# One more gate chunk before the shift columns, two shift tiles fewer on TensorE, a two-product low-rank chunk, and a query chunk behind linear attention

## The chip, the core and the metric

The kernel runs on one core of a Trainium2 chip. Its time is the device time of one execution in microseconds (us). Three runs of the kernel before took 2047.29, 2050.56 and 2052.04 us, with 2050.56 as their median. The trace is that of one further execution, which took 2051.18 us; from its first to its last instruction, its span, it took 2049.4 us.

The profile's names for the engines: PE is TensorE's matmul side and PEld its load of stationary blocks; DVE is VectorE, ACT is ScalarE, POOL is GpSimd, and SP is SyncE, which only issues DMAs here. Each engine works through its own instructions in the order in which they were written.

## What is computed

The reference is a trunk of two layers on 640 tokens, 128 of a context and 512 of a latent grid, with a model width of 2048. Both groups of tokens use the same weights; they differ in the conditioning vector that modulates them.

```python
for l in range(DEPTH):
    shift, scale, gate = modulation(c, ada_w[l], ada_b[l])     # silu(c) @ w + b, in three
    h = rms_norm(x, norm_g[l]) * (1.0 + scale) + shift
    if l % 2 == 0:      # even layer: attention || bidirectional gated linear attention (GLA)
        y, side = even_mixer(h, w_in_even[e], ...)
    else:               # odd layer: neighbourhood attention || spatial gating
        y, side = odd_mixer(h, w_in_odd[o], ...)
    x = x + gate * (y @ w_out[l])
y = rms_norm(x, final_norm_g)
```

In the even layer, `h @ w_in_even` gives eight attention queries, two keys and two values of 128 columns, the queries, keys and values of four GLA heads, 32 low-rank columns `r` from which the GLA gates `log_sigmoid(r @ wg + bg) / 16` are made, and 2048 gate columns; the mixers' output is multiplied with the SiLU of the gate columns. Everything is float32.

## The kernel before

**The matmuls.** Activations lie transposed: 16 blocks of 128 features by 640 tokens. A float32 product is made of three matmuls in a rounded type: both operands are split into a high part, which is the operand rounded, and a low part, which is the rest, and high x high, high x low and low x high are added up in a PSUM bank. The high parts are rounded by ACT (`acth`, `whi`), the low parts subtracted by POOL or DVE (`actl`, `wlo`). A *chunk* is 128 output columns of a weight: 16 blocks of the contraction, two halves of 320 tokens, three products, so 96 matmuls, all issued through one helper at L449 (`mm_k` calls it). The *shift* of the modulation is not added to the activations; it stands beside them as two extra columns (one of the context, one of the latent tokens), so that the second half of a chunk has 322 columns and the shift's part comes out as two columns of the bank. A chunk's result leaves its bank by three DVE instructions: `arena<-bank,rstd 128x320` for each half, which multiplies by the tokens' reciprocal norm, and `bc<-bank 128x2` for the two shift columns. The two halves alternate every four blocks and three banks rotate over them, so the bank of a chunk's first half is wanted again 24 matmuls after that half is complete.

**The start.** The modulation of layer 0 has to be made first. Its scales are 16 *tiles*: two 512 KB loads each (`Y<-ada`, `more<-ada`), 32 records in the profile at L1605 (16 matmuls with a stationary block of 32 columns, each in two records), a copy, and a matmul `small,adas` of two columns. The shifts' 16 blocks are made in two ways. `BOTH` = 8 of them are such tiles too. The other 8 are done by row: 256 KB loads (`raw<-ada_s`, four to a block, with a ring of five buffers), which DVE multiplies with the conditioning rows and adds up (`adas,old<-raw,bank`, a custom instruction with the read-out of its sum), once for each of the two conditioning vectors; some of the second are done by POOL (`prod<-raw,mixrow`) and ACT. When the last row is in, a few DVE additions, a rounding on ACT and a subtraction on DVE (`actl<-old,acth`, L1255) give the two shift columns. Until they exist, PE can work on chunks whose shift part is made elsewhere: the first `FIRST` = 6 gate chunks (columns 320 in both halves; their shift part is reduced from other loads, `gateT`, on DVE) and the first half of the low-rank chunk. The order of PE's work here is: matmuls of the gate chunks with tiles in between, the low-rank chunk's first half, then a transposition `ident,old` of the shifts and the low-rank chunk's second half, the first with 322 columns.

**After it** come the 16 GLA chunks (k, q and two v for each of four heads), each evacuated into elementwise work of its head: on DVE four `TENSOR_SCALAR`, a product, a scan over the tokens, another product and a backward scan, in an order that the planner sets; a gate chunk (gate 14) is the filler while the last GLA head ends, then k, v and the eight queries of the attention with the attention heads in between, and the other gate chunks. The out-projection of each layer and the chunks of the odd layer are done in pairs with Strassen's method, whose sums of weight or activation blocks are made by ACT, DVE and POOL. At the border to layer 1 the new activations are normed, scaled (`rs<-rs,A`, `adas<-adas,A`), rounded (`acth`) and split (`actl`) while PE works.

**What sets the order.** A planner in the program simulates the engines when the kernel is built: the class `Pace` holds a cost for each kind of instruction, generators of side work are spawned, and after every few matmuls `tick` lets them write their next instructions. `until` makes a generator wait until an operand would be there, `calm(x)` until ACT and DVE have at most so much work queued, and `need` makes PE's side run the others until a flag is set. Nothing of that runs on the chip; it fixes the order of each engine's queue. In `units`, where a chunk's matmuls are written, it stands so:

```python
for j in range(k, k + 4):
    if p[half] is not done:
        self.mm_k(c, j, [(p[half], half)], k0)
    if j % 2:
        self.tick(2)
```

Of the kernel before, what the change touches and what calls it, by code (L numbers as in the profile page):

```python
# [50 lines left out]
LEAD, FIRST = 1, 6  # L51
CUT, AGAIN, KEPT = 384, (10, 2), (8, 0)
BOTH = 8
# [192 lines left out]
class Trunk:  # L246
# [425 lines left out]
    def strassen_jobs(self, c1, c2, last, unit):  # L672
# [25 lines left out]
        add = lambda o, a, b, op: ("add", lambda: (piece(o), piece(a), piece(b)), op, 4 in (o, a, b))  # L698
# [9 lines left out]
        if ns == ALL:  # L708
            after = {("A12", 8): [add1], ("S1", 5): [add2], ("S2", 5): [add3], ("S4", 5): [add4]}
            assert all(t in [k + m for k, m in self.blocks_of(ns, f)] for f, t in after)  # L710
        else:
            after = {("A12", 6): [add1, add2], ("S1", 6): [add3], ("S2", 6): [add4]}
# [41 lines left out]
    def wpump(self, force=False):  # L754
# [107 lines left out]
    def mm_k(self, c, k, outs, first=0, last=KT - 1, r=0):  # L862
# [4 lines left out]
        todo = []  # L867
# [117 lines left out]
    def spair(self, c1, c2):  # L985
# [70 lines left out]
        end = self.steps(c1, c2)[-1]  # L1056
        for key in self.steps(c1, c2):
            f = key[1]
            if len(key) == 3 and key[0] == c1:
# [10 lines left out]
            elif f == "S1":  # L1070
                plus(full(xa), x)
                ev1(xa, None)
                self.drop(xa)
                v = take()
                self.need("T124")
                product(v, full, f, tt(0))
            elif f == "S2":
                product(t, full, f, tt(1))
                x = copy(half(t))
                plus(x, half(v))  # L1080
            elif f == "S4":
# [4 lines left out]
                self.drop(xb)  # L1086
            elif f == "S3":
# [2041 lines left out]
```

## Time and profile before

| | |
|---|---|
| median of three runs | 2050.56 us (2047.29 to 2052.04) |
| the profiled execution | 2051.18 us, span 2049.4 us |
| mean granted TensorE clock | 0.996 |
| busy: PE, DVE, ACT, POOL | 2012.4, 1356.0, 1098.7, 1362.9 us |
| matmul records | 14255 |
| moved by DMA | 344.13 MB, 168 GB/s on average |

How to read it: busy time is the time in which an engine has an instruction in work. Matmuls overlap, so one that is listed with 0.31 us starts 0.15 us after the one before it; the distance of two starts, not the listed duration, is what a matmul costs. In the waits, a row names the engine that waits with its instruction's operand and line, behind the arrow what ended the wait, and then the sum in us, the number of waits and the longest. In the timeline's rows stand the start and the duration in us, the instruction with its shapes, and in brackets the idle time before it with what ended it. In the table of stretches of time, each engine's busy time (and instructions) stands in the order PE, PEld, DVE, ACT, POOL, then the granted clock, the share of time that the 16 DMA engines were busy, and GB/s.

### The profile page before, as it was taken

What the parts mean: (1) busy time and instruction counts of PE and PEld (TensorE: products, weight loads), DVE (VectorE), ACT (ScalarE), POOL (GpSimd) and SP (SyncE); (2) the same over time, 40 slices, a digit from 0 to 9 for tenths busy, and PEclk for the clock granted to TensorE, in tenths of its full rate; (3) what the DMA queues carried; (4) which work ended last, traced back from release to release, by engine and by line L of the source; (5) the groups of instructions that cost most, each with busy time, mean ns of one, the idle gap of its engine ahead of it and who ended that gap; (6) DMA issues with size and microseconds to landing.
All of it is one profiled execution on the core that took longest, in us unless ns stands there. A gap on an engine that the chain in (4) does not pass through costs nothing.

```text
span 2049.4 us, 40331 instructions
## 1 busy us (share of the span) xinstructions
PE 2012.4 (98%) x14255; PEld 1976.9 (96%) x14255; DVE 1356.0 (66%) x3175; ACT 1098.7 (54%) x2430; POOL 1362.9 (67%) x1096
## 2 busy tenths in 40 slices
PE   8999999999999999999999999999999999999997
PEld 6899999999999999999989999999999999999997
DVE  4656677476557666898577787656665677568444
ACT  5445555445564766544465444565565654455443
POOL 5555465446556555798755777766766688878884
PEclk9999999999999999999999999999999999999999
DMA  9965433336456455577534434444344354265437
GB/s 376 400 208 163 143 112 102 121 119 185 156 184 215 148 179 179 174 242 230 186 107 138 134 126 132 133 132 130 120 147 126 120 174 154 91 216 194 144 98 277
DMA packets 234316, 344.13 MB, mean 168 GB/s; under 512 B 22049, under 2 KB 139649, under 8 KB 234113
## 3 DMA queue, kind: packets, MB, share of 16 engines
q1 hardware_dynamic: 232912, 340.38, 50.7%
q8 instruction: 112, 1.84, 0.4%
q10 hardware_dynamic: 1200, 1.17, 0.2%
q14 instruction: 92, 0.75, 0.1%
HBM read 304.99 MB, written 33.85 MB: 165 GB/s over the span
## 4 chain that ended last, share of the span: by engine, by line
PE 87%; DMA 6%; DVE 3%; ACT 2%; issue 1%; POOL 1%; SPq 0%; DVEq 0%; POOLq 0%; ACTq 0%
PE bank L449 84%; PE bank L454 2%; DMA more<-ada 1%; DMA Y<-ada 1%; DVE bank L219 1%; DVE arena L219 1%; DVE Y L219 1%; DMA arena<-yT_dram 1%; PE bank L1605 0%; DMA Y<-xT 0%; ACT acth L219 0%; DMA wraw<-w_even 0%; DMA wraw<-w_out 0%; DVE rs L219 0%; DMA rawx<-ada_g 0%
## 5 line engine op out<-in xcount | busy, mean ns | idle before, releaser
L449 PE MATMUL bank<-acth,whi 128*128 128x320 f32 (+3 forms) x3072 | 941.0, 318 | 6.8 <-DVE bc L219 2.8
L449 PE MATMUL bank<-actl,whi 128*128 128x320 f32 (+3 forms) x3072 | 917.0, 310 | 1.3 <-POOL actl L219 1.3
L449 PE MATMUL bank<-acth,wlo 128*128 128x320 f32 (+3 forms) x3072 | 915.6, 310 | 0.0
L219 POOL TENSOR_TENSOR wlo<-wraw,whi 128x512 fp32r<-128x512 f32 (+2 forms) x415 | 531.3, 1290 | 395.3 <-ACT whi L219 360.4
L449 PEld LDWEIGHTS bank<-acth,whi 128*128 128x128 f32 (+1 forms) x3072 | 569.1, 188 | 14.7 <-issue 4.1
L449 PEld LDWEIGHTS bank<-actl,whi 128*128 128x128 f32 (+1 forms) x3072 | 569.6, 188 | 3.5 <-POOL actl L219 1.5
L449 PEld LDWEIGHTS bank<-acth,wlo 128*128 128x128 f32 (+1 forms) x3072 | 568.6, 188 | 0.8 <-POOL wlo L219 0.6
L219 POOL TENSOR_TENSOR wlo<-rs,whi 128x384 fp32r<-128x384 f32 (+2 forms) x370 | 457.7, 1262 | 111.4 <-ACT whi L219 78.5
L219 ACT ACTIVATE whi<-wraw 128x512 fp32r<-128x512 f32 (+2 forms) x425 | 245.8, 586 | 164.1 <-PE bank L449 85.2
L219 ACT ACTIVATE whi<-rs 128x384 fp32r<-128x384 f32 (+2 forms) x370 | 191.9, 536 | 100.8 <-PE bank L449 45.7
L449 PE MATMUL bank<-eh,whi 128*128 128x322 f32 (+1 forms) x666 | 209.5, 314 | 0.0
L449 PE MATMUL bank<-el,whi 128*128 128x322 f32 (+1 forms) x666 | 206.4, 310 | 0.0
L449 PE MATMUL bank<-eh,wlo 128*128 128x322 f32 (+1 forms) x666 | 206.3, 310 | 0.0
L219 POOL TENSOR_TENSOR prod<-adas,mixrow 128x512 f32<-128x512 f32 x93 | 121.1, 1313 | 50.6 <-ACT prod L219 32.4
L219 DVE TENSOR_TENSOR bank<-bank,sums 128x320 f32<-128x320 f32 (+1 forms) x148 | 70.1, 495 | 95.8 <-ACT sums L219 47.9
L449 PEld LDWEIGHTS bank<-eh,whi 128*128 128x128 f32 x666 | 125.4, 188 | 0.0
L449 PEld LDWEIGHTS bank<-eh,wlo 128*128 128x128 f32 x666 | 125.4, 188 | 0.0
L449 PEld LDWEIGHTS bank<-el,whi 128*128 128x128 f32 x666 | 125.3, 188 | 0.0
L219 DVE CUSTOM_DVE_ANT_0 adas<-adas,bank,part 128x512 bf16<-128x512 f32 x146 | 108.6, 744 | 22.6 <-DMA adas<-ada 15.7
L219 POOL TENSOR_TENSOR wlo<-adas,whi 128x512 fp32r<-128x512 f32 x62 | 80.2, 1300 | 44.0 <-ACT whi L219 43.5
L219 ACT ACTIVATE sums<-bank 128x320 f32<-128x320 f32 (+1 forms) x111 | 48.2, 434 | 103.6 <-PE bank L449 97.4
L219 DVE CUSTOM_DVE_ANT_0 adas<-adas,bank 128x512 bf16<-128x512 f32 x107 | 73.2, 684 | 13.6 <-DMA adas<-ada 5.2
(287 smaller groups left out, 3057.6 us busy)
## 6 DMA issues: line engine op xcount, KB each, us to landing
wraw<-w_even SPq DMA_DIRECT2D x176, 256.0 KB, 3.3
rs<-w_odd SPq DMA_DIRECT2D x150, 256.0 KB, 3.3
adas<-ada SPq DMA_DIRECT2D x128, 256.0 KB, 3.8
adas<-ada_g SPq DMA_DIRECT2D x64, 256.0 KB, 3.8
rs<-w_out SPq DMA_DIRECT2D x60, 256.0 KB, 3.7
adas<-w_odd SPq DMA_DIRECT2D x50, 256.0 KB, 3.8
Y<-ada SPq DMA_DIRECT2D x24, 512.0 KB, 7.7
more<-ada SPq DMA_DIRECT2D x24, 512.0 KB, 7.8
```

Source lines behind the costliest of these rows:

```text
L219: return f(*args, **kw)
L449: self.nc.tensor.matmul(out, lhsT, rhs, start=start, stop=stop, **kw)
L454: self.nc.tensor.transpose(out, in_, self.ident[:k, :k])
```

## The change

1. `FIRST` goes from 6 to 7: gate chunk 14 is now one of those without a shift column and runs in the start.
2. `BOTH` goes from 8 to 6: two of the shift tiles leave PE, and the shifts of 10 blocks instead of 8 are reduced from row loads: 40 loads of 256 KB instead of 32, and 4 of 512 KB fewer.
3. The low-rank chunk's weight has its 32 columns four times in a stationary block of 128 columns, one of them replaced by the low part. Two matmuls replace three: the block with the activations' high part (128 columns), and 32 high columns with their low part. The chunk has 64 matmuls instead of 96; the 128 rows of its result take over the parts that the small gate product needs (`gla_wg`, `gla_rank`).
4. Query chunk 0 takes the filler's place behind the GLA chunks, in a third buffer beside the gates'; attention head 0 is spawned as soon as the first value chunk is done.
5. `units` ticks after every block of the contraction, with 1 and 2 in turn, where it ticked 2 after every second.
6. In the Strassen pairs that end a run of pairs, the products come in another order (S2, S1, S3, S4, A22, or S3 ahead of the second plain block), the sums with them, and one sum is written in two halves.
7. At the border, the split of a block waits for `calm(1.5)` while the last block isn't rewritten yet, where it waited for `calm(3.0)`.
8. The reciprocal root of a GLA head's norm is written out, with an `until` between ACT's and DVE's part.

```diff
-LEAD, FIRST = 1, 6
+LEAD, FIRST = 1, 7
-BOTH = 8
+BOTH = 6
@@ strassen order
         if self.count[c1] == ALL:
-            return names("A11", "A12", "S1", "S2", "S4", *(("S3", "A22") if c1 in self.ends else ("A22", "S3")))
-        return [*names("A11"), (c1, PLAIN, 0), *names("A12", "S1", "S2", "S4"), (c2, PLAIN, 0), *names("S3", "A22")]
+            return names("A11", "A12", *(("S2", "S1", "S3", "S4", "A22") if c1 in self.ends else ("S1", "S2", "S4", "A22", "S3")))
+        last = [*names("S3"), (c2, PLAIN, 0)] if c1 in self.ends else [(c2, PLAIN, 0), *names("S3")]
+        return [*names("A11"), (c1, PLAIN, 0), *names("A12", "S1", "S2", "S4"), *last, *names("A22")]
...
         if m < M:
-            raw = raw[:, :, None, :].to_broadcast([128, n, M // m, m])
-            hi, lo = (x.rearrange("p a (b c) -> p a b c", c=m) for x in hl)
-        nc.scalar.activation(hi, raw, AF.Copy)
+            hi, lo = hi.rearrange("p a (b c) -> p a b c", c=m), hi[:, :, 0:m]
+            nc.scalar.activation(hi, raw[:, :, None, :].to_broadcast([128, n, M // m, m]), AF.Copy)
+            hi, hl = lo, [hl[0], hl[0]]
+        else:
+            nc.scalar.activation(hi, raw, AF.Copy)
...
+            if m < M:
+                n = h.shape[1]
+                self.mm(p[:M, :n], hi, h, start=k == first, stop=k == last, skip_group_check=True)
+                self.mm(p[:m, :n], hi[:, m : 2 * m], l, start=False, stop=k == last, skip_group_check=True)
+                continue
             todo += [(0, p, hi, h, k == first, False), (1, p, hi, l, False, False), (2, p, lo, h, False, k == last)]
...
-                    if j % 2:
-                        self.tick(2)
+                    self.tick(1 + j % 2)
...
-            yield from self.calm(self.calms[1])
+            yield from self.calm(self.calms[1] if f"{ready}:{order[-1]}" in self.flags else 1.5)
...
-        self.rsqrt(rs, sq, sq2)
+        self.act(rs, sq, AF.Ln)
+        self.act(rs, rs, AF.Exp, scale=-0.5)
+        yield from self.until(rs)
+        nc.vector.scalar_tensor_tensor(sq2, rs, -0.5, rs, ALU.mult, ALU.mult)
...
-        add(d["w_rb"], 96, True, None, lazy("vt", rows=96, then=lambda x: self.spawn(self.gla_rank(x))))
+        add(d["w_rb"], 128, True, None, lazy("vt", then=lambda x: self.spawn(self.gla_rank(x))))
...
-        gp_first(14)
+        add(wE[0], 128, True, None, lazy("hq", SC, pre=("gla_elem3",), then=lambda x: L.update(q0=x)))
...
                 self.spawn(work())
+                if kv == 0:
+                    self.spawn(self.even_head(0, L["q0"], L["k0"], v, L["sw"].next(), "eq0"))
...
-            for h in range(4 * kv, 4 * kv + 4):
+            for h in range(4 * kv or 1, 4 * kv + 4):
```

Three places in the engines' orders. In these rows an instruction's line, its kind, what it writes and reads, and its shape are given; x4 means four of it in a row.

**SP, the last loads of the tiles.** Before:

```order
L492 DMA raw_297<-crow_b 128x512
L492 DMA raw_298<-ada_s 128x512
L492 DMA raw_299<-ada_s 128x512
L492 DMA Y<-ada 128x1024
L492 DMA more_126<-ada 128x1024 x3
L492 DMA wraw<-w_even 128x512
L492 DMA wraw<-w_rb 128x128
L492 DMA raw_300<-ada_s 128x512
```

With the change:

```order
L492 DMA wraw<-w_even 128x512
L492 DMA more_126<-ada 128x1024 x2
L492 DMA raw_296<-ada_s 128x512
L492 DMA wraw<-w_even 128x512
L492 DMA Y<-ada 128x1024 x2
L492 DMA raw_297<-ada_s 128x512
L492 DMA raw_298<-ada_s 128x512
L492 DMA raw_299<-ada_s 128x512
```

Both pieces hold the last load of a tile (`more_126<-ada` before, `Y<-ada` with the change). Up to it the queue has issued 42.75 MB before and 39.86 MB with the change. Behind it stand 14 rows of `ada_s` and two of `crow_b` (the conditioning rows) before, and 23 and four with the change. On PE, 188 matmuls of 320 columns stood between the last tile's `small,adas` and the transposition `ident,old` of the shifts, and now 292; in all, 620 matmuls of 320 columns stood ahead of that transposition, and now 702.

**DVE, the third GLA head (head 2) and the evacuation of the next chunk** (`bank_68` and `bank_69` are its halves). Before:

```order
L219 TENSOR_SCALAR Y<-bank_72,small 128x320
L219 TENSOR_TENSOR Y<-Y,arena_1683 128x640
L219 SCALAR_TENSOR_TENSOR arena_1683<-arena_1683,Y 128x640
L219 TENSOR_TENSOR Y<-Y 128x640
L219 SCALAR_TENSOR_TENSOR Y<-arena_1683,Y 128x640
L219 TENSOR_TENSOR arena_1683<-bank_68,rstd 128x320
L219 TENSOR_SCALAR bc_3507<-bank_68 128x2
L219 TENSOR_TENSOR arena_1683<-bank_69,rstd 128x320
```

With the change:

```order
L219 TENSOR_SCALAR Y<-bank_72,small 128x320
L219 TENSOR_TENSOR Y<-Y,arena_1768 128x640
L219 SCALAR_TENSOR_TENSOR arena_1768<-arena_1768,Y 128x640
L219 TENSOR_TENSOR arena_1768<-bank_68,rstd 128x320
L219 TENSOR_SCALAR bc_3600<-bank_68 128x2
L219 TENSOR_TENSOR arena_1768<-bank_69,rstd 128x320
L219 TENSOR_TENSOR arena_1768<-arena_1768 128x640 x2
L219 TENSOR_TENSOR Y<-Y 128x640
```

The evacuation stood behind the second scan (the second `SCALAR_TENSOR_TENSOR`); it now stands ahead of the product `Y<-Y` and of that scan. On PE, 49 matmuls lay between the head's last small gate product and the bank's next use, and now 40.

**ACT, the border to layer 1** (`rs`, `adas`: blocks that are scaled; `eh`: a rounding of another sum, which waits for DVE). Before:

```order
L219 ACTIVATE acth<-rs_8045 128x640
L219 ACTIVATE whi<-wraw 128x512
L219 ACTIVATE eh_8043<-bank_69 128x320
L219 ACTIVATE adas<-adas,A_97 128x128
L219 ACTIVATE adas<-adas,A_97 128x512
L219 ACTIVATE acth<-adas 128x640
```

With the change:

```order
L219 ACTIVATE rs_8048<-rs_8048,A_97 128x128
L219 ACTIVATE rs_8048<-rs_8048,A_97 128x512
L219 ACTIVATE acth<-rs_8048 128x640
L219 ACTIVATE whi<-wraw 128x512
L219 ACTIVATE adas<-adas,A_97 128x128
L219 ACTIVATE adas<-adas,A_97 128x512
L219 ACTIVATE acth<-adas 128x640
```

The `eh` no longer stands between the two blocks, and the scaling of the `rs` block, which DVE did before for this block (`rs<-rs,A`), is on ACT.

More of the change, by code (lines that the diff above doesn't have):

```diff
@@ L709, in strassen_jobs @@
             after = {("A12", 8): [add1], ("S1", 5): [add2], ("S2", 5): [add3], ("S4", 5): [add4]}
+            if c1 in self.ends:
+                after = {("A11", 8): [add1], ("A12", 4): [add2], ("S2", 5): [add3], ("S1", 5): [add(4, 3, 2, ALU.subtract, (0, 4))], ("S1", 8): [add(4, 3, 2, ALU.subtract, (4, 8))]}
             assert all(t in [k + m for k, m in self.blocks_of(ns, f)] for f, t in after)
@@ L866, in mm_k @@
         hi, lo = (x[:, i, :] for x in self.wget((c, u, r)))
-        todo = []
+        todo, m = [], w.shape[2]
         for p, half in outs:
@@ L1056, in spair @@
         end = self.steps(c1, c2)[-1]
+        done = set()
         for key in self.steps(c1, c2):
             f = key[1]
+            done.add(key)
             if len(key) == 3 and key[0] == c1:
@@ L1069, in spair @@
                 product(xa, full, f, M(x1))
[L1070 to L1080, printed above, removed]
+            elif f in ("S1", "S2"):
+                if xa:
+                    plus(full(xa), x)
+                    ev1(xa, None)
+                    self.drop(xa)
+                    xa = None
+                    self.need("T124")
+                if f == "S1":
+                    v = take()
+                    product(v, full, f, tt(0))
+                else:
+                    product(t, full, f, tt(1))
+                    x = copy(half(t))
+                if {(c1, "S1"), (c1, "S2")} <= done:
+                    plus(x, half(v))
             elif f == "S4":
@@ L1086, in spair @@
                 self.drop(xb)
+                if (c1, "S3") in done:
+                    x = copy(full(t))
+                    self.drop(t)
             elif f == "S3":
@@ L1091, in spair @@
                     self.spawn(self.unfold(ns), first=True)
+                if xb is None:
+                    continue
                 x = copy(full(t))
@@ L2002, in gla_wg @@
         nc, wg, ws = self.nc, self.L["wg"], self.L["wgs"]
-        self.dma(wg[0:96, :], self.d["gla_wgp"][:, h])
-        yield from self.until(wg[0:96, :])
-        nc.scalar.activation(ws[0:96, :], wg[0:96, :], AF.Copy)
-        nc.vector.tensor_tensor(ws[32:64, :], wg[32:64, :], ws[32:64, :].bitcast(F32), ALU.subtract)
+        self.dma(wg, self.d["gla_wgp"][:, h])
+        yield from self.until(wg)
+        nc.scalar.activation(ws, wg, AF.Copy)
+        nc.vector.tensor_tensor(ws[64:96, :], wg[64:96, :], ws[64:96, :].bitcast(F32), ALU.subtract)
         self.flags.add(f"wg{h}")
@@ L2013, in gla_rank @@
         yield from self.until(x)
-        nc.scalar.activation(r[0:96, :], x[0:96, :], AF.Copy)
-        nc.vector.tensor_tensor(r[64:96, :], x[64:96, :], r[64:96, :].bitcast(F32), ALU.subtract)
+        nc.scalar.activation(r, x, AF.Copy)
+        nc.vector.tensor_tensor(r[96:128, :], x[96:128, :], r[96:128, :].bitcast(F32), ALU.subtract)
         self.flags.add("r")
@@ L2447, in flag @@
             return lambda: self.flags.add(f)
-        def gp_first(i):
-            ev = self.gate(self.yt(i), None)
-            def evac(pa, pb):
-                ev(pa, pb)
-                if pb is not None:
-                    self.flags.add(f"gp{i}")
-            add(wE[28 + i], 128, True, None, evac)
         for i in range(FIRST):
@@ L2467, in open_gla @@
             self.gate_pool = tc.tile_pool(name="gp", bufs=1)
-            gx = self.t(self.gate_pool.__enter__(), [128, 2, T], "gx2")
-            L["gx"] = Ring([gx[:, i, :] for i in range(2)])
-            self.arena(15.2)
+            gx = self.t(self.gate_pool.__enter__(), [128, 3, T], "gx3")
+            L["gx"], L["hq"] = Ring([gx[:, i, :] for i in range(2)]), Ring([gx[:, 2, :]])
+            self.arena(14.2)
             self.rp = tc.tile_pool(name="rp", bufs=1)
@@ L2480, in open_gla @@
             L["KI"] = [Y[:, 5, :], self.take()]
-            for n in ("q", "k", "vt", "scanm"):
+            L["q"] = gx[:, 2, :]
+            for n in ("k", "vt", "scanm"):
                 L[n] = self.take()
@@ L2559, in open_att @@
             self.close_arena()
-            self.arena(16.55)
-            L["hq"] = self.take(T, 3)
+            self.arena(15.55)
+            L["hq"].list += self.take(T, 2).list
             L["hk"] = Ring([Y[:, 6, :], self.take()])
```

8 lines of the change are left out of this document (5 added, 3 removed).

## The prediction

> **What bounds the kernel now.** I read the page first: its busy shares and the chain of work that ended last, then the timeline's last row of PE.
>
> ```profile
> PE 2012.4 (98%) x14255; PEld 1976.9 (96%) x14255; DVE 1356.0 (66%) x3175; ACT 1098.7 (54%) x2430; POOL 1362.9 (67%) x1096
> PE 87%; DMA 6%; DVE 3%; ACT 2%; issue 1%; POOL 1%; SPq 0%; DVEq 0%; POOLq 0%; ACTq 0%
> 2036.47 0.70 PE L449 MATMUL bank<-Y,rawx 128*128 128x256 f32 x2 [0.23 <-ACT Y L219]
> ```
>
> PE has 37 us of its 2049.4 us without a matmul, and the chain runs over it for 87%. Such a kernel gets shorter in three ways only: fewer or shorter matmuls, the 37 us, or stretches in which the clock isn't whole. Some 12 us of the 37 are the tail, behind PE's last matmul at 2036.47. So I read next, stretch by stretch, where PE is not full (columns: PE, PEld, DVE, ACT, POOL busy, clock, DMA share, GB/s).
>
> ```profile
> 20.00:117.00 97.00, 91.49 (x1122) 81.57 (x1121) 56.01 (x129) 51.16 (x115) 55.94 (x41) 1.00 1.00 390
> 117.00:146.00 29.00, 29.00 (x198) 28.63 (x197) 23.14 (x59) 15.51 (x37) 20.42 (x18) 1.00 0.52 162
> ```
>
> Up to 117 us the DMA engines are full at 390 GB/s and PE waits for them; from then on PE is full. That border falls on the last shift tile. Which waits PE has in the whole program, the table of waits tells (us in total, times, longest):
>
> ```profile
> PE bank L1605 <- DMA Y<-ada: 8.3, 4, 5.1
> PE bank L449 <- DVE bc L219: 2.8, 2, 2.0
> PE bank L1605 <- DMA more<-ada: 1.4, 2, 1.2
> ```
>
> The first row's longest, 5.1, is the very first load and stays. The tiles' other DMA waits are 8.3 + 1.4 - 5.1 = 4.6 us. The rest are single stalls, and each belongs to a place.
>
> **Matmuls that go: the low-rank chunk.** Its 96-column matmuls start 0.147 us apart (144.09 to 145.42, nine steps), the 128-column ones too (117.41 to 117.85, three steps):
>
> ```profile
> 115.04 1.08 PE L1605 MATMUL bank<-more,cond 128*32 128x128 f32 x32
> 116.05 0.41 PE L449 MATMUL bank<-acth,whi 128*128 128x320 f32 x1
> 117.04 0.28 PE L449 MATMUL bank<-small,adas 128*128 128x2 f32 x2
> 117.17 0.39 PE L449 MATMUL bank<-acth,whi 128*128 128x320 f32 x1
> 117.41 0.32 PE L449 MATMUL bank<-actl,whi 128*128 128x320 f32 x1
> 117.85 0.31 PE L449 MATMUL bank<-actl,whi 128*128 128x320 f32 x1
> 144.09 0.31 PE L449 MATMUL bank<-acth,wlo 128*96 128x320 f32 x1
> 145.42 0.31 PE L449 MATMUL bank<-acth,wlo 128*96 128x320 f32 x1
> 145.56 0.27 PE L454 MATMUL bank<-ident,old 128*32 128x128 f32 x1
> 146.54 0.31 PE L449 MATMUL bank<-acth,whi 128*96 128x322 f32 x1
> ```
>
> So the number of stationary columns doesn't show at this width, and 32 matmuls fewer are 32 x 0.147 = 4.7 us. The new 32-column ones with 320 columns have no row; between nothing (they cost as much as the others) and a gain (32 columns load faster, but the moving 320 columns stay), I take the others' 0.147, since 96 against 128 columns made no difference. The term is -4.7 us, all of it on PE's path, as this chunk runs with PE full.
>
> **Two tiles leave PE.** From the rows above a tile is 116.05 - 115.04 = 1.01 us, and its `small,adas` 117.17 - 117.04 = 0.13: 1.14 us, so -2.3 us for two.
>
> **The gate chunk in the start.** Gate 14 goes into the start and query 0 takes its place behind the GLA: 96 matmuls against 96, nothing by themselves. But the chunk gives PE work where it waited for tiles. The last load of a tile is issued after 42.75 MB before and after 39.86 MB now; at the 390 GB/s of 20 to 117 us these 2.89 MB are 7.4 us, so the last tile ends at 117.17 - 7.4 = 109.8. From there 292 matmuls lead to the shifts' transposition: 109.8 + 292 x 0.147 = 152.7. If the waits stayed as they are, the transposition would come at 145.56 - 2.3 + 82 x 0.147 = 155.3 (82 more matmuls stand ahead of it). The difference, -2.6 us, is what PE's waits for tiles shrink by. Bounds: nothing, if PE's own work sets the tiles' pace, and -4.6, all those waits; I take -2.6, which lies in the middle and is the one that follows from bytes.
>
> **Do the shift columns come in time?** This is the change's debit. Before, they are ready at 145.2 for a use at 146.54:
>
> ```profile
> L492 SPq DMA_DIRECT2D more<-ada x24: 327/328/1134, 3.9 to 106.1; - x24
> L492 SPq DMA_DIRECT2D raw<-ada_s x32: 327/328/907, 28.5 to 137.3; - x32
> L219 DVE TENSOR_TENSOR YB<-YB,bank x30: 469/482/489, 36.7 to 139.8; 128x320 f32<-128x320 f32 x30
> 140.92 0.75 DVE L219 CUSTOM_DVE_ANT_0 adas<-raw,bank,old 128x512 bf16<-128x512 f32 x1
> ...
> 141.71 0.75 DVE L219 CUSTOM_DVE_ANT_0 adas<-raw,bank,old 128x512 bf16<-128x512 f32 x1
> 145.02 0.20 DVE L1255 TENSOR_TENSOR actl<-old,acth 128x32 fp32r<-128x32 f32 x1 [0.30 <-ACT acth L1254]
> ```
>
> DVE has 13 reductions more in the start (61 for 48), 0.79 us each (140.92 to 141.71), 10.3 us. Behind the last tile, its order shows 31 reductions and 12 additions `YB<-YB,bank` of 0.48 us where it had 19 and 7; the other work there is the same. That is 12 x 0.79 + 5 x 0.48 = 11.9 us more. Before, the last tile's end and the ready shifts are 145.2 - 117.17 = 28.0 us apart, so I expect 109.8 + 28.0 + 11.9 = 149.7, while PE comes to its use at 152.7 + 1.0 = 153.7. The cover is the added chunk, and 4 us of it are left. The row loads aren't short: DMA is half idle in 117 to 146 us. I cost this part at nothing, with +5.7 as the other end (third rival).
>
> **The stall in GLA head 2.** Before, the next chunk's evacuation stands behind the backward scan in DVE's queue:
>
> ```profile
> 340.20 1.85 DVE L219 TENSOR_TENSOR Y<-Y 128x640 f32<-128x640 f32 x1
> 342.08 2.46 DVE L219 TENSOR_TENSOR_SCAN Y<-arena,Y 128x640 f32<-128x640 f32 x1
> 344.46 0.46 DVE L219 TENSOR_TENSOR arena<-bank,rstd 128x320 f32<-128x320 f32 x1
> 345.04 0.41 PE L449 MATMUL bank<-acth,whi 128*128 128x320 f32 x1 [2.03 <-DVE bc L219]
> 345.00:350.00 5.00, 4.96 (x24) 4.92 (x25) 4.16 (x7) 3.47 (x9) 0.00 (x0) 0.66 0.04 16
> 350.00:355.00 5.00, 5.00 (x36) 5.00 (x35) 4.68 (x5) 4.90 (x8) 2.78 (x2) 1.00 0.18 52
> ```
>
> PE waits 2.0 us for the bank, and in the next 5 us the granted clock is 0.66: 24 matmuls for the 36 of the stretch after, 5 x 0.34 = 1.7 us lost. With the change the evacuation precedes the product and the scan, 1.85 + 2.46 = 4.3 us earlier, while the bank's next use comes 9 matmuls, 1.3 us, earlier. That leaves 4.3 - 1.3 - 2.0 = 1.0 us to spare, so I take -2.0 and -1.7 (bounds: 0, if the scan's own result is then late for PE, and -3.7). What is late next is the backward scan, which moves back by the evacuation's 1 us and its neighbours.
>
> [...]
>
> **The border to layer 1.** Two waits stand 0.9 us apart, and the clock falls again:
>
> ```profile
> 1057.94 0.57 PE L449 MATMUL bank<-acth,whi 128*128 128x322 f32 x2 [0.94 <-ACT acth L219]
> 1059.79 0.90 PE L449 MATMUL bank<-actl,whi 128*128 128x322 f32 x2 [1.28 <-POOL actl L219]
> 1048.88 3.09 DVE L219 TENSOR_SCALAR rs<-rs,A 128x128 f32<-128x128 f32 x2
> 1052.01 0.74 ACT L219 ACTIVATE acth<-rs 128x640 fp32r<-128x640 f32 x1 [1.65 <-DVE rs L219]
> 1055.78 0.44 ACT L219 ACTIVATE eh<-bank 128x320 fp32r<-128x320 f32 x1 [2.52 <-DVE bank L219]
> 1056.12 1.00 ACT L219 ACTIVATE adas<-adas,A 128x128 f32<-128x128 f32 x2
> 1060.00:1065.00 5.00, 5.00 (x25) 5.00 (x26) 3.94 (x4) 3.49 (x8) 3.86 (x3) 0.68 0.28 97
> ```
>
> ACT reaches the `adas` block late: it waits 1.65 us for DVE's slow scaling of `rs` (3.09 us; on ACT the like of it takes 1.00) and 2.52 us behind an `eh` that DVE hasn't fed. In the new order the scaling of `rs` is on ACT and no `eh` stands in between, so up to 4.2 us fall out of a chain that made PE wait 0.94 + 1.28 = 2.2 us; with the low clock, 5 x 0.32 = 1.6. I take -3.8 (bounds 0 and -3.8: at worst another block's sum, moved here, is late instead).
>
> **Finer ticks, the Strassen order, head 0 earlier, the written-out root.** No row of PE's waits names the border sums that part 6 of the change moves, so their order alone hides nothing that PE waits for: 0. The finer ticks put every side instruction one block earlier or later, and a queue that fits one order by 0.2 us can stall in another. Head 0 of the attention enters with such stalls already:
>
> ```profile
> 531.71 0.49 PE L449 MATMUL bank<-arena 128*128 128x128 f32 x2 [1.31 <-DVE arena L219]
> 534.18 0.33 PE L454 MATMUL bank<-ident,arena 128*128 128x128 f32 x1 [0.67 <-ACT arena L219]
> ```
>
> They are 2.0 us; the head is spawned earlier, but its first matmuls stand as far behind the spawn, so I leave them in and charge one more stall of that size, +2.0 (bounds -2.0 and +4.0).
>
> **The sum.** -4.7 - 2.3 - 2.6 - 3.7 - 3.8 + 2.0 = -15.1 us against the profiled execution's 2051.2, of which 2049.4 is its span: 2036.1. That execution lies 0.6 over the median of the runs, so 2035.5.
>
> **The rivals.**
> *The waits only move.* PE's work and the filled start count (4.7 + 2.3 + 2.6 = 9.6 us), while the planner's new order makes as much stalling as it takes away: 2050.6 - 9.6 = 2041.0. For it: DVE and POOL are two thirds busy, and each stall came from one instruction in a queue. Against: two of the stalls have a named cause that the new order doesn't have. 0.23.
>
> *The low clock isn't the waits' doing.* If the two half-clock stretches come by themselves, or fall elsewhere, 1.7 + 1.6 stay: 2035.5 + 3.3 = 2038.8. For it: there are PE waits of over 1 us in the start, where the clock stays 1.00. Against: both stretches follow right behind the two places with about 2 us of waiting. 0.14.
>
> *The shifts come late.* If the 27 row loads behind the last tile's go at the pace of before's last 16, one every (137.3 - 106.1) / 16 = 1.95 us (106.1 and 137.3 are the last issues of a tile load and of a row), their last is issued at 106.1 - 7.4 + 27 x 1.95 = 151.4, and the shifts are ready 145.2 - 137.3 = 7.9 us later, 159.3, 5.7 after PE's 153.7; with a low clock of 1.7 behind it that is 7.4 lost: 2042.9. Against: that pace was DVE's own in a stretch with other work. 0.11.
>
> *Slower: the rows keep the pace of the whole start.* 32 rows took 28.5 to 137.3, 3.5 us each. At that pace 40 rows are issued by 28.5 + 39 x 3.5 = 165.0, the shifts are ready at 172.9, PE waits 19.2, and with 1.7 of low clock the time is 2056.4. It decides against the change from a wait of about 13 us on. For it: five buffers, and the same SP queue that carries the weights. Against: that average lies in the stretch with DMA at 1.00, which ends with the tiles. 0.05.
>
> **How the numbers follow.** The forecast has 0.47, the rivals 0.23, 0.14, 0.11 and 0.05. The range is 2029 to 2046: below, the forecast without the charge of 2.0, with all 4.6 of the tiles' waits gone and the attention's 2.0 too (2035.5 - 6.0 = 2029.5); above, late shifts with one more stall (2042.9 + 2.0) and a little. No change means within 0.2%, 4.1 us, about what a measurement of this kernel can tell: faster is under 2046.5. The forecast gives 0.96 of its chance to that, the moved waits 0.88, the clock 0.95, late shifts 0.7, the last none: 0.45 + 0.20 + 0.13 + 0.08 = 0.86. Slower gets the last rival's share and a little: 0.05; the same 0.09.
>
> **What would show it.** Right: 32 low-rank matmuls fewer at 0.147 us; the last tile at about 110 us and the transposition near 153 with no PE wait before it; no `bc` wait of 2 us and a clock of 1.00 in GLA head 2; no `actl` wait at the border. Wrong: a wait of PE for `actl` at L1275 (the shifts) of several us, DMA still full beyond 115 us, new waits of 1 to 2 us in the GLA or the attention that weren't there, or the half clock in as many stretches as before.

## The result, and the profile after

The changed kernel took 2030.59 us (median of four runs, 2029.96 to 2031.87), the kernel before 2048.93 us beside it (2045.09 to 2052.04). The ratio is 0.9917, with a 95% interval of 0.9903 to 0.9930: 18.3 us by the medians, 14 to 20 us by the interval. The forecast was 15.1 us, to 2035.5, with a range of 2029 to 2046. One execution of the kernel before in a later session, 2142.75 us at a granted clock of 0.874, is left out everywhere below.

The profiled execution of the changed kernel has a span of 2029.3 us, 20.1 less than that of before. The profile page's busy time, and the chain of work that ended last:

```profile
PE 2001.4 (99%) x14155; PEld 1966.2 (97%) x14155; DVE 1373.9 (68%) x3211; ACT 1105.3 (54%) x2445; POOL 1371.6 (68%) x1102
PE 92%; DMA 4%; DVE 1%; issue 1%; ACT 1%; POOL 0%; SPq 0%; DVEq 0%; POOLq 0%; ACTq 0%
```

PE has 100 matmul records fewer and 28 us without a matmul instead of 37. Of the 20.1 us, 9.1 are time without a matmul and 11.0 are busy time; before has two stretches of 3.4 us at half clock that the changed kernel doesn't have, which make about 3.4 of the 11.0, so that some 7.6 are matmuls that went. In the table of PE's waits, the border's `actl` and `acth` are gone; two waits for `bc` are still there, the longest 1.2 us:

```profile
PE bank L1625 <- DMA Y<-ada: 8.7, 6, 5.3
PE bank L449 <- DVE bc L219: 1.9, 2, 1.2
PE bank L449 <- POOL wlo L219: 1.5, 4, 0.8
PE bank L449 <- DVE YB L219: 1.4, 2, 1.0
PE bank L449 <- ACT adas L219: 0.8, 2, 0.4
```

The start, in the timeline: the last tile's `small,adas`, the low-rank chunk's matmuls in their two forms, the transposition of the shifts, and on DVE the last sum of the shifts (`old`, which the transposition reads) and the end of the shift columns:

```profile
108.40 0.28 PE L449 MATMUL bank<-small,adas 128*128 128x2 f32 x2
150.38 0.31 PE L449 MATMUL bank<-acth,whi 128*128 128x320 f32 x1
150.52 0.31 PE L449 MATMUL bank<-actl,whi 128*32 128x320 f32 x1
152.29 0.31 PE L449 MATMUL bank<-actl,whi 128*32 128x320 f32 x1
152.43 0.27 PE L454 MATMUL bank<-ident,old 128*32 128x128 f32 x1
151.06 0.29 DVE L219 TENSOR_TENSOR old<-old,small 128x10 f32<-128x10 f32 x2
151.66 0.19 DVE L1275 TENSOR_TENSOR actl<-old,acth 128x32 fp32r<-128x32 f32 x1 [0.30 <-ACT acth L1274]
```

The forecast had 109.8 for the last tile, 152.7 for the transposition and 149.7 for the shifts. A 32-column matmul took as long here as one of 128 columns: from 150.38 to 152.29 there are 13 steps of 0.147 us.

GLA head 2 and the border are full, with a whole clock:

```profile
340.00:345.00 5.00, 5.00 (x36) 5.00 (x36) 2.68 (x6) 3.49 (x8) 4.79 (x3) 1.00 0.19 66
345.00:350.00 5.00, 5.00 (x36) 5.00 (x36) 4.97 (x8) 3.99 (x8) 3.26 (x3) 1.00 0.23 65
1035.00:1040.00 5.00, 5.00 (x34) 4.84 (x34) 3.62 (x5) 4.90 (x11) 4.45 (x4) 1.00 0.39 139
1040.00:1045.00 5.00, 5.00 (x34) 4.84 (x33) 3.50 (x6) 4.28 (x9) 3.87 (x3) 1.00 0.03 7
```

To see where the time went, I cut both traces at places behind which the same number of projection matmuls still follows, counted back from the last one. Then a stage holds the same number of matmuls in every kernel, and the start carries what was removed. (With seven gate chunks in the start, the cuts around the GLA lie one chunk earlier in the GLA's own order, and the query behind it stands where the filler stood.) In us, from the first matmul to the last projection matmul (the runs of the experiments are told below):

| kernel | start | GLA | attention, gates | first out-projection | border, layer 1's begin | layer 1 | last out-projection, begin | rest |
|---|---|---|---|---|---|---|---|---|
| before | 169.8 | 332.1 | 272.1 | 210.7 | 168.6 | 596.0 | 118.1 | 162.4 |
| changed | 159.6 | 330.3 | 270.3 | 209.2 | 160.4 | 596.0 | 121.1 | 162.4 |
| low-rank alone | 169.2 | 331.0 | 268.8 | 210.6 | 167.5 | 595.9 | 118.1 | 162.4 |
| before, `BOTH` = 6 | 173.4 | 332.1 | 270.1 | 211.6 | 167.3 | 595.9 | 118.3 | 162.4 |
| changed, `BOTH` = 8 | 162.4 | 330.1 | 271.5 | 209.5 | 161.7 | 595.9 | 119.1 | 162.9 |
| parts 1 to 4 | 156.6 | 327.3 | 269.9 | 210.0 | 169.4 | 596.0 | 118.9 | 162.5 |
| parts 5 to 8 | 167.6 | 333.9 | 271.4 | 210.5 | 160.2 | 595.9 | 118.9 | 162.9 |
| changed, old ticks | 158.6 | 327.4 | 270.3 | 209.1 | 160.5 | 595.9 | 119.0 | 162.9 |
| changed, old Strassen order | 156.7 | 330.3 | 270.4 | 208.9 | 161.4 | 595.9 | 121.5 | 162.4 |
| changed, `calm(3.0)` | 157.8 | 330.2 | 270.9 | 210.8 | 165.0 | 595.9 | 117.9 | 162.6 |
| changed, old ticks and old Strassen order | 157.2 | 327.4 | 270.1 | 209.4 | 162.0 | 595.9 | 120.5 | 162.9 |

So the start gave 10.2 us, the border 8.2, the GLA only 1.8, the attention 1.8, the first out-projection 1.5, and the last out-projection took 3.0. Three kernels share the changed kernel's order in the start (the changed one, that with the old Strassen order and that with `calm(3.0)`), and theirs took 159.6, 156.7 and 157.8: one profiled start is good to about 3 us, while the stages from the GLA on repeat to a few tenths where the order is the same.

Runs of the kernel before spread over 9 us in the four sessions that have several (2043.1 to 2052.2, with medians of 2045.7 to 2048.9), and a single one in a fifth took 2053.69; its profiled execution, 2051.18, lies near the upper end; the changed kernel's four lie within 2. So some of the 20.1 us between the two spans is that spread.

### The profile page after: what moved, and what is told of

It reads as the page before. It is cut to its first block, busy times and chain, and to the rows that moved or that the text cites. A ratio compares the mean times of both kernels' runs of the same rounds, so it can differ in the third digit from the quotient of the medians.

```text
span 2029.3 us, 40239 instructions
## 1 busy us (share of the span) xinstructions
PE 2001.4 (99%) x14155; PEld 1966.2 (97%) x14155; DVE 1373.9 (68%) x3211; ACT 1105.3 (54%) x2445; POOL 1371.6 (68%) x1102
## 3 DMA queue, kind: packets, MB, share of 16 engines
q10 hardware_dynamic: 1200, 1.17, 0.2%
## 4 chain that ended last, share of the span: by engine, by line
PE 92%; DMA 4%; DVE 1%; issue 1%; ACT 1%; POOL 0%; SPq 0%; DVEq 0%; POOLq 0%; ACTq 0%
PE bank L449 89%; PE bank L454 2%; DMA more<-ada 1%; DMA Y<-xT 1%; DMA raw<-ada_s 1%; DVE Y L219 1%; DMA wraw<-w_even 1%; PE bank L1625 1%; POOL wlo L219 0%; DMA Y<-ada 0%; DVE arena L219 0%; DMA Y<-yT_dram 0%; ACT arena L219 0%; DVE rs L219 0%; DMA rs<-w_out 0%
## 5 line engine op out<-in xcount | busy, mean ns | idle before, releaser
L449 PE MATMUL bank<-acth,whi 128*128 128x320 f32 (+2 forms) x3072 | 939.1, 318 | 3.4 <-DVE bc L219 1.9
L449 PE MATMUL bank<-acth,wlo 128*128 128x322 f32 (+3 forms) x3040 | 904.5, 309 | 0.0
L449 PEld LDWEIGHTS bank<-acth,whi 128*128 128x128 f32 x3072 | 569.0, 188 | 11.3 <-issue 2.8
L449 PEld LDWEIGHTS bank<-acth,wlo 128*128 128x128 f32 x3040 | 562.5, 188 | 0.4 <-POOL wlo L219 0.2
L449 PE MATMUL bank<-eh,whi 128*128 128x322 f32 (+1 forms) x666 | 209.5, 315 | 0.0
```

The lines of the kernel that those rows point to most:

```text
L449: self.nc.tensor.matmul(out, lhsT, rhs, start=start, stop=stop, **kw)
```

## The experiments

**The low-rank chunk alone.** The weight's lines, `mm_k`, and the small gate product's operands of the change (part 3) on the kernel before:

```diff
+            if m < M:
+                n = h.shape[1]
+                self.mm(p[:M, :n], hi, h, start=k == first, stop=k == last, skip_group_check=True)
+                self.mm(p[:m, :n], hi[:, m : 2 * m], l, start=False, stop=k == last, skip_group_check=True)
+                continue
...
-        add(d["w_rb"], 96, True, None, lazy("vt", rows=96, then=lambda x: self.spawn(self.gla_rank(x))))
+        add(d["w_rb"], 128, True, None, lazy("vt", then=lambda x: self.spawn(self.gla_rank(x))))
```

> The kernel before with the two-product low-rank chunk alone (part 3). Theory: 32 matmuls of 0.147 us go, 4.7 us, and as the order of DVE's queue now has GLA head 2's evacuation ahead of the backward scan, the 2.0 us wait and the low clock behind it (1.7 us) go too: a span of about 2049.4 - 8.4 = 2041, with the border's waits at 1058 and 1060 us still there. Rival 1: the work counts and nothing else, 2044.7. Rival 2: a matmul with 32 stationary columns does not take the pace of the others (0.20 us instead of 0.147 would give 32 x 0.05 = 1.7 back), 2046.4.

This kernel doesn't compute part of the even layer's output as the reference does, and why was not found; it has 14223 matmul records, 32 fewer than before, as meant, and only its time is read. Measured: 2043.71 us against 2046.40 (medians), ratio 0.9991 [0.9980, 1.0002], no difference that can be told; the profiled span is 2044.3, the number of rival 1, but not for its reason. The matmuls keep the pace of 0.147 us, so rival 2 falls. But the start is shorter by 0.6 us only, though 4.7 us of matmuls left it. PE now comes to the shifts before DVE has them:

```profile
147.23 0.28 PE L454 MATMUL bank<-ident,old 128*32 128x128 f32 x1 [1.67 <-DVE old L219]
148.20:151.60 3.40, 3.40 (x15) 2.79 (x14) 0.00 (x0) 0.63 (x1) 1.27 (x1) 0.50 0.44 110
345.73 0.42 PE L449 MATMUL bank<-acth,whi 128*128 128x320 f32 x1 [1.51 <-DVE bc L219]
345.00:350.00 5.00, 4.27 (x30) 4.26 (x31) 4.40 (x10) 3.63 (x8) 1.29 (x1) 1.00 0.54 178
```

A wait of 1.67 us, and 3.4 x 0.50 = 1.7 us of low clock behind it, give 3.4 of the 4.7 back. The shorter chunk by itself runs into the end of DVE's shift chain; in the kernels with the seventh gate chunk PE doesn't wait there. The GLA is 1.1 us shorter, not 3.7. DVE's order has the evacuation ahead of the backward scan, as the theory said, and PE still waits for `bc` in head 2, 1.51 us instead of 2.03, with a whole clock (the last two rows); another `bc` wait, of 0.79 us, stands at 329.

**Fewer tiles without the added chunk.**

```diff
-BOTH = 8
+BOTH = 6
```

> The kernel before with BOTH = 6 alone: two tiles fewer on TensorE, the shifts of 10 blocks by rows, but still 6 gate chunks ahead of them. Theory: the seventh gate chunk is the cover of the longer DVE work. The last tile load is issued after 39.6 MB instead of 42.7, so the last tile ends near 109; 230 matmuls later, at 143, PE wants the shift columns, which are ready near 149 (151.9 in the changed kernel, less 5 additions of 0.48 us): a wait for actl of about 5.5 us and 1.7 us of low clock, against 2.3 us of tiles and 1 to 3 us of filling: about 2 to 4 us slower than before, 2052 of span. Rival: the rows are early enough without the chunk: no wait, 2045 of span.

Measured: 2052.46 us against 2046.40, ratio 1.0030 [1.0012, 1.0047]: a little slower, as the theory said. The last tile ends at 108, PE wants the shifts at 142.8, and they come 6 us later:

```profile
148.78 0.40 PE L454 MATMUL bank<-ident,old 128*32 128x128 f32 x1 [5.97 <-DVE old L219]
143.00:149.00 6.00, 0.22 (x1) 0.10 (x1) 4.90 (x18) 2.77 (x9) 4.06 (x5) 0.66 0.28 93
149.00:154.00 5.00, 5.00 (x26) 4.95 (x26) 0.19 (x1) 0.94 (x3) 1.28 (x1) 0.72 0.44 85
```

So the prediction's third rival (shifts that come late) is what the two tiles fewer bring without `FIRST` = 7: a wait of 6.0 us (5.5 expected) and 5 x 0.28 = 1.4 us of low clock.

**The tiles back in the changed kernel.**

```diff
-BOTH = 6
+BOTH = 8
```

> The changed kernel with BOTH = 8 again: seven gate chunks, eight shift tiles. Theory: the filling of PE's waits comes from the fewer bytes ahead of the last tile load (43.0 MB here, 39.9 in the changed kernel), so that 2.3 us of tiles and about 2.9 us of filling come back: 2029.3 + 5.2 = 2034.5 of span, the last tile ending near 117. Rival: the added gate chunk alone gives PE work in its waits for DMA, and only the tiles' 2.3 come back: 2031.6.

Measured: 2033.20 us, ratio to before 0.9942 [0.9928, 0.9957]; the profiled span is 2032.7. The last tile ends at 117.3, as the bytes ahead of its load say (43.0 MB; before, 42.75 MB and 117.17). The start takes 162.4 us, 4.4 more than the mean of 158.0 of the three kernels with the changed start; the tiles are 2.3 of it. The rest, 2.1, is nearer to the theory's 2.9 than to nothing, but single starts differ by as much. PE's waits in the start say more. Before, and in this run:

```profile
PE bank L449 <- ACT adas L219: 2.6, 4, 1.1
PE bank L1625 <- DMA Y<-ada: 8.4, 4, 5.3
PE bank L449 <- ACT adas L219: 0.7, 2, 0.4
```

Without the first load, the waits for the tiles' loads and for their `adas` are 4.6 + 2.6 = 7.2 us before, 3.4 + 0.8 = 4.2 in the changed kernel, and here, with the bytes of before, 3.1 + 0.7 = 3.8. In the kernel before with `BOTH` = 6 they are 2.7 + 2.6 = 5.3. So the added chunk fills the waits by itself, as the rival has it; the medians, 2.6 us above the changed kernel's (of another session), are near the rival's 2.3 too.

**Parts 1 to 4 without the ordering parts, and parts 5 to 8 without the others.** The first run undoes, in the changed kernel, the ticks, the Strassen order, `calm(1.5)` and the written-out root; the second puts these four into the kernel before. The edits of the first:

```diff
-                    self.tick(1 + j % 2)
+                    if j % 2:
+                        self.tick(2)
...
-            yield from self.calm(self.calms[1] if f"{ready}:{order[-1]}" in self.flags else 1.5)
+            yield from self.calm(self.calms[1])
...
-        self.act(rs, sq, AF.Ln)
-        self.act(rs, rs, AF.Exp, scale=-0.5)
-        yield from self.until(rs)
...
+        self.rsqrt(rs, sq, sq2)
...
-            return names("A11", "A12", *(("S2", "S1", "S3", "S4", "A22") if c1 in self.ends else ("S1", "S2", "S4", "A22", "S3")))
+            return names("A11", "A12", "S1", "S2", "S4", *(("S3", "A22") if c1 in self.ends else ("A22", "S3")))
...
```

> The change's parts 1 to 4 without its changes of ticks, Strassen order, calm and root (parts 5 to 8). Theory: the terms of work and start add up as in the changed kernel, 4.7 + 2.3 + 2.9 = 9.9, and the stalls stay those of before, since DVE's order has GLA head 2's evacuation behind the backward scan again and the border's rs scaling is on DVE again: 2049.4 - 9.9 = 2039.5 of span, with waits at head 2, the attention's entry and the border. Rival: the larger part of the stalls goes with the parts 1 to 4 because they shift the meeting of DVE's and PE's queues: 2032 to 2034.

> The kernel before with the change's parts 5 to 8 alone (finer ticks, Strassen order, calm(1.5), written-out root). Theory: the border's 8 us are theirs and the start stays as it is (the last tile near 117 us, the shifts' transposition near 145.5): 2049.4 - 8.2 = 2041 of span, with the GLA neither won nor lost as a whole. Rival: the border becomes free only together with parts 1 to 4, since the run of these alone was already 19 of 20 us faster: 2046 to 2049.

Measured: parts 1 to 4 took 2032.90 us, ratio 0.9944 [0.9929, 0.9958]; parts 5 to 8 took 2045.20, ratio 0.9985 [0.9973, 0.9998]. The two together, 0.9929, are near the whole change's 0.9917. The profiled spans are 2030.3 and 2041.8. The first is 9 us below its theory, nearer to the rival's 2032 to 2034. The border has not gone free with parts 1 to 4: the stages show 169.4 us there, as before, and the same three waits stand in its timeline, 19.3 us earlier, with the low clock behind them:

```profile
1020.58 0.78 PE L449 MATMUL bank<-acth,whi 128*128 128x322 f32 x2 [2.27 <-DVE Y L219]
1038.60 0.57 PE L449 MATMUL bank<-acth,whi 128*128 128x322 f32 x2 [0.94 <-ACT acth L219]
1040.45 0.90 PE L449 MATMUL bank<-actl,whi 128*128 128x322 f32 x2 [1.29 <-POOL actl L219]
1040.00:1045.00 5.00, 4.55 (x22) 4.55 (x23) 3.29 (x4) 4.11 (x8) 3.87 (x4) 0.67 0.21 66
```

What it won beyond its theory lies in the start (156.6), in the GLA (327.3, 4.8 less than before, without any wait) and in the attention (2.2 less). That undoes one of my explanations: this kernel has GLA head 2's evacuation behind the backward scan, as before, and PE doesn't wait:

```profile
341.96 1.49 DVE L219 TENSOR_TENSOR_SCAN Y<-arena,Y 128x640 f32<-128x640 f32 x1
343.37 0.47 DVE L219 TENSOR_TENSOR arena<-bank,rstd 128x320 f32<-128x320 f32 x1
```

The scan is the same, but its 1.49 us stand against 2.46 in before, and the chain and the chunk meet at another moment. Together with the low-rank chunk alone, which has the evacuation ahead of the scan and waits 1.51 us, that shows that the place of the evacuation in the queue neither suffices to lose that wait nor is needed for it. Parts 5 to 8 alone set the border free (160.2) and leave the GLA longer than before (333.9).

**The ticks, the Strassen order and `calm(1.5)`, each undone in the changed kernel, and the first two together.** The edits are the single pieces of the diff above.

> The changed kernel with the old ticks (part 5 undone). Theory: the finer ticks cost more in the GLA than they bring; the run of parts 1 to 4 has no wait in the GLA at all, where the changed kernel waits 1.2 us in head 1 and runs 4 us longer up to the attention. Without them: 2029.3 - 4 = 2025 of span, and no wait for bc near 275 us. Rival: the finer ticks are what took away the attention's entry waits (2.3 us) and those at 827 and 856 us (1.5): these come back, 2029.3 + 3.8 = 2033, or 2029 if both hold.

> The changed kernel with the old order of Strassen products (part 6 undone). Theory: the new order is the source of the new waits in the last out-projection (for bc at 1809.7, for wlo between 1845 and 1848), which cost 3.2 us from there to the end: 2026 of span without them. Rival: they come from elsewhere and the order takes away the waits of before at 1135 and 1152 us: those 2.1 us come back, 2031.4.

> The changed kernel with calm(3.0) at the border again (part 7 undone). Theory: this one number keeps the slow scaling of rs off DVE and the eh out from between ACT's blocks; with it undone, the waits at the border (for acth 0.9, for actl 1.3, and the low clock behind them) come back, 6.2 us with the wait before them: 2035.5 of span. Rival: the border is free because PE comes to it at another time or in another Strassen order: 2029 to 2030.

> The changed kernel without its finer ticks and without its order of Strassen products: parts 1 to 4, calm(1.5) and the written-out root remain. Theory: the GLA and the last out-projection lose their new waits and the border stays free, so the two gains add up: 2029.3 - 4 - 3.2 = 2022 of span, faster than the changed kernel. Rival: each of the two parts has a stall that it takes away, and what is won is lost there: 2029.

Measured against before's 2045.75 in the same session (median of six runs):

| | median us | ratio [95%] | span |
|---|---|---|---|
| old ticks | 2025.15 | 0.9902 [0.9887, 0.9918] | 2023.3 |
| old Strassen order | 2031.06 | 0.9929 [0.9914, 0.9945] | 2027.9 |
| `calm(3.0)` | 2032.90 | 0.9939 [0.9921, 0.9957] | 2030.9 |
| old ticks and old Strassen order | 2028.20 | 0.9915 [0.9900, 0.9931] | 2025.3 |

*The ticks.* The theory holds: without the finer ticks the GLA takes 327.4 us instead of 330.3, and the attention and the first out-projection keep their gains (270.3 and 209.1), so the rival falls. The changed kernel's new wait is in head 1, where two products stand ahead of the evacuation; it is 1.17 to 1.19 us in the changed kernel, that with the old Strassen order and that with `calm(3.0)`, and 1.59 with `BOTH` = 8:

```profile
269.60 2.74 DVE L219 TENSOR_TENSOR_SCAN Y<-arena,Y 128x640 f32<-128x640 f32 x1
272.27 3.68 DVE L219 TENSOR_TENSOR arena<-arena 128x640 f32<-128x640 f32 x2
275.88 0.48 DVE L219 TENSOR_TENSOR arena<-bank,rstd 128x320 f32<-128x320 f32 x1
276.48 0.42 PE L449 MATMUL bank<-acth,whi 128*128 128x320 f32 x1 [1.19 <-DVE bc L219]
```

With the old ticks those products stand behind the evacuation's first part. That kernel, 2025.15 us against before's 2045.75, was the fastest that ran; its runs (2023.98 to 2027.00) lie below all four of the changed kernel, though these were taken in another session, so the difference of some 5 us has no interval of its own.

*The Strassen order.* The theory falls: with the old order, the begin of the last out-projection takes 121.5 us, as long as with the new one, and its waits stand at the same places. The border is 1.0 us longer, with a wait for `Y` of 0.36 us. With the ticks undone as well, the last out-projection's begin takes 120.5 us and the wait for `Y` is 0.76 us; the span of 2025.3 lies between the theory's 2022 and the rival's 2029. What makes this stage 118 or 121 us was not found: the kernel with `calm(3.0)` has 117.9, though its edit is at another place of the program. Each edit of the planner's rules changes the queues far behind it.

*`calm(1.5)`.* With 3.0, DVE has the slow `rs` scaling again, and the waits for `actl` are back:

```profile
1030.54 3.09 DVE L219 TENSOR_SCALAR rs<-rs,A 128x128 f32<-128x128 f32 x2
1041.45 0.56 PE L449 MATMUL bank<-actl,whi 128*128 128x322 f32 x2 [0.90 <-POOL actl L219]
1044.20 0.56 PE L449 MATMUL bank<-actl,whi 128*128 128x322 f32 x2 [0.71 <-POOL actl L219]
1040.00:1045.00 5.00, 3.38 (x20) 2.77 (x20) 2.36 (x2) 4.91 (x11) 4.15 (x3) 1.00 0.15 51
```

The border takes 165.0 us, 4.6 more than in the changed kernel (6.2 expected), and the clock stays whole this time. So this number is worth more than half of the border's 8.2 us. The rest goes with the other ordering parts: the wait for `Y` ahead of it (1.25 us before, 2.27 in the run of parts 1 to 4) isn't there with `calm(3.0)` either. The two waits for `adas` at the end of this stage (0.45 and 0.79 us before, none in the changed kernel) are back with `calm(3.0)`, 0.40 and 0.60 us.

**When does the clock fall?** PE's waits were lengthened on purpose, in the changed kernel with the old ticks: ahead of a chunk's first matmul, DVE multiplies the bank by one, several times.

```diff
+                    n = {32: 6, 34: 8, 36: 9, 38: 10, 40: 12, 42: 14}.get(c, 0)
+                    for _ in range(0 if half else n):
+                        self.nc.vector.tensor_scalar(p[0][:, 0:HT], p[0][:, 0:HT], 1.0, None, ALU.mult)
```

> The changed kernel with the old ticks, and six places between 560 and 780 us at which DVE multiplies the bank that a chunk is to begin in by one, 6, 8, 9, 10, 12 and 14 times (about 0.45 us each), ahead of the chunk's first matmul, so that PE waits there by growing times of some 0.7 to 4.3 us. Theory: a wait of 2 us or more is followed by a stretch of 3.4 us at half the clock, 1.7 us lost, one below about 1.3 us is not. [...]

Its one run took 2078.76 us. The waits came out longer than meant, 4.46 to 8.15 us, and behind all six the granted clock was 0.50; that says nothing of shorter waits, so a second run had one to four multiplications at eleven chunks.

> As the run with six long holds, whose waits came out at 4.5 to 8.2 us (each followed by a low clock), but with one to four multiplications of the bank at eleven chunks, for waits between 0.5 and 3.5 us. Theory: waits from about 2 us on are followed by a stretch of lower clock, those below 1.3 us are not, and the place of the step lies between. [...]

Its one run took 2062.71 us. Its waits were 1.79, 1.52, 1.49, 1.85, 3.67, 3.11, 1.69, 3.64, 2.06, 2.57 and 2.76 us. Half clock followed the 1.85, 3.67, 3.11, 3.64, 2.06 and 2.57, and not the 2.76. Two of them, each with the stretches of 3.4 us around it:

```profile
641.25 0.39 PE L449 MATMUL bank<-acth,whi 128*128 128x322 f32 x1 [1.85 <-DVE bank L219]
639.00:642.40 3.40, 1.55 (x11) 1.32 (x10) 3.26 (x9) 2.23 (x6) 2.10 (x2) 1.00 0.70 233
642.40:645.80 3.40, 3.40 (x14) 3.40 (x13) 2.59 (x9) 0.00 (x0) 1.70 (x2) 0.50 0.43 123
803.92 0.42 PE L449 MATMUL bank<-acth,whi 128*128 128x322 f32 x1 [2.76 <-DVE bank L219]
799.40:802.80 3.40, 1.76 (x13) 1.50 (x11) 3.29 (x9) 3.06 (x7) 2.66 (x3) 1.00 0.58 190
802.80:806.20 3.40, 2.28 (x15) 2.28 (x16) 3.34 (x5) 1.09 (x4) 3.10 (x3) 1.00 0.43 149
```

Neither theory holds as it was put: it isn't the length of a wait alone. From the granted clock in stretches of 1 us, the halvings begin at 642.38, 662.86, 690.16, 734.54, 758.42 and 778.90 us. Their distances are 6, 8, 13, 7 and 6 times 3.413 us, to 0.02. The two halvings of the kernel before, at 346.42 and 1059.80 us, are 209 such steps apart, and each of them lasts 3.413 us in its trace. So the halvings seen here lie on a grid of 3.413 us. Laid on that grid, the wait of 1.85 us fell into one cell, with PE idle for 54% of it; the one of 2.76 was cut by a cell's border into 1.63 and 1.13, 48% and 33%. In this run, the longest idle time within one cell that had no consequence is 1.66 us (of the 1.69 us wait), the shortest that had one 1.85. In the kernel before, between the first 20 us and the tail, the two cells with more than 1.85 us (2.03 and 2.2) are followed by half clock. Other cells, laid on their own kernel's grid in the same way, show that the step isn't sharp: one of 1.66 us (the border in the run of parts 1 to 4, 0.94 and 0.72 of the 1.29) and one of 1.67 in the start of the low-rank chunk alone are followed by half clock, while one of 1.61 us at before's attention (0.97 and 0.64 of the waits of 1.31 and 0.67) is not. So my estimate from these cells is a step at about half a cell, 1.7 us; what else decides near it is open.

## Why the prediction came out as it did

The size and the sign were right, and the range held, but the sum fits better than its terms: the border gave 4.4 us more than its term, the attention and the first out-projection 3.3 that had no term, the GLA 1.9 less, and the last out-projection lost 3.0. That these errors partly cancel, to 3.2 us by the medians (18.3 against 15.1), is luck. By its own steps:

- **The low-rank chunk, -4.7.** Right: 13 steps of 0.147 us for both new forms. That it pays by itself was wrong to imply: alone it gave nothing that the runs can tell.
- **The tiles, -2.3, and the filling, -2.6.** The start gave 10.2 us in the pair of profiles, less 4.7 and 2.3 leaves 3.2 for the filling (with the mean of the three starts of that order, 11.8, it would be 4.8), and the waits for tiles shrank by 3.0. So the size fits. The reason that it was sized by, the fewer bytes ahead of the last tile, is not what the runs show: with those bytes back, and the added chunk, the waits are as short. And 1.8 of the 3.0 are waits for `adas`, which the prediction had not counted. The step from bytes to the last tile (109.8, measured end 108.5) and on to the transposition (152.7, measured 152.43) held.
- **The shifts in time, 0.** Right, by less than I said: 151.85 for a use at 153.13, a margin of 1.3 us instead of 4. The transposition, where the two kernels with late shifts wait, is nearer: it starts at 152.43, and `old` is ready at 151.35. The chain behind the last tile took 43.4 us, not 39.9. Without the chunk it costs 6.0 us of waiting, which was the third rival's mechanism.
- **GLA head 2, -3.7.** The wait and its low clock went, but the reason given doesn't hold by itself: the run of parts 1 to 4 has the evacuation behind the scan and doesn't wait, the low-rank chunk alone has it ahead and waits 1.51 us. What is left is the moment at which the head's chain and PE's next use of the bank meet, and no run singles that out. And the GLA as a whole gave 1.8 us: the finer ticks put a wait of 1.2 us into head 1 and make the GLA 2.9 us longer than it is without them.
- **The border, -3.8.** The mechanism was right and the size too small: the stage gave 8.2. I had counted two waits and the clock behind them, and left out the 1.25 us wait for `Y` at 1039.91, which is gone with `calm(3.0)` too, and the two waits for `adas` behind it. The Strassen order, put at nothing, is worth about 1 us here: with the old one the stage is 1.0 us longer.
- **The charge, +2.0.** It stood for new stalls, and its place was wrong. The attention's entry, which I had left in, lost its waits of 2.0 us, and the first out-projection its 0.76 and 0.40 at 828 and 857; the stalls came in GLA head 1 and in the last out-projection (3.0 us). That the Strassen order made the latter was my first reading, and the run with the old order refutes it.
- **The rivals.** That the waits only move gave too small a gain, 9.6 us: waits and low clock that went elsewhere are about as much again. That the low clock isn't the waits' doing falls with the lengthened waits, but so does a plain length: the 1.7 us behind a wait of 2 us are a matter of where it lies on the grid, as the wait of 2.76 us shows. Before's 2.03 us in head 2 lay in one cell as a whole (343.01 to 346.42), and so did 2.2 us of the border's 0.94 and 1.28. The slower rival, rows at the whole start's pace, was far off: the rows behind the tiles came fast enough, the last of them issued at 143.9 us instead of 165.0.

What stays open: what sets 118 or 121 us in the last out-projection, what removed the wait in head 2, and why the kernels with six gate chunks in the start spread over 4 to 9 us from run to run (2041.1 to 2049.4 with parts 5 to 8, too), those with seven, of which only four runs each exist, over 2 to 5. The margin of the shifts doesn't tell the two apart: at the transposition it is 0.85 us before and 1.1 in the changed kernel.

## What to carry to other kernels

Before work is taken off the engine that bounds a stretch, look what else ends there: here a side chain finished 1 us ahead, and a saving of 4.7 us brought nothing that the runs can tell until that chain had cover. Where a planner writes the queues, every edit also reshuffles far places, so run the parts of a change singly and compare stage by stage; one of eight parts here lost 2.9 us in one stage inside a gain of 18. A short wait of a busy TensorE cost its length here, and up to 1.7 us more where at least 1.66 us of it lay in one 3.413 us cell of the grid of the clock's halvings.

## What the runs showed of the hardware

The halvings of the granted clock lay on a grid of 3.413 us: six within 137 us in the run with short waits, to 0.02 us, and two in the kernel before, 209 steps apart, each 3.413 us long. Between 556 and 810 us of that run, and between the first 20 us and the tail of the kernel before, every cell at whole clock in which PE idled for 1.85 us or more was followed by a cell at half the clock; with 1.66 us both were seen (none behind the run's wait of 1.69, half clock at the border in the run of parts 1 to 4). A wait of 2.76 us that a border of the grid cuts into 1.63 and 1.13 left the clock whole. And 32 stationary columns cost what 128 did when 320 columns passed: 0.147 us in the changed kernel, from 150.38 to 152.29.
